# Asking for the first prompt tile's queries and keys during the decoding batch's attention

## The chip, the core and the metric

The kernel runs on one core of one Trainium2 chip. The metric is the device time of one execution in microseconds. The core's engines run side by side and wait for each other through semaphores: TensorE (PE, whose weight loads are listed apart as PEld), VectorE (DVE), ScalarE (ACT), GpSimd (POOL), and SyncE (SP), whose queue issues nearly all DMAs of this kernel in program order.

## The reference

One layer of a streaming encoder is computed for a prompt of 2048 tokens and for a decoding batch of 8 sequences with 16 tokens each. Cut to what matters here:

```python
qm, km, vm, om, ip, fp, qa, ka, va = split_in(x @ w_in)      # one input projection
hm, C1, n1, m1 = mlstm_chunkwise(qm, km, vm, logi, logf, C0, n0, m0, mchunk)
qa = rope(qa.reshape(B, T, A_Q_HEADS, A_HEAD_DIM), pos)      # 8 query heads, 2 key heads of 64
ka = rope(ka.reshape(B, T, A_KV_HEADS, A_HEAD_DIM), pos)
ha = swa_prompt(qa, ka, va, attn_sinks)                      # prompt: window of 128 before the own chunk
ha = swa_step(qa, ka, va, k_cache, v_cache, attn_sinks)      # decoding batch: against its cache
mix = jnp.concatenate([hm, ha], axis=-1) @ w_out
h = layer_norm(DEEPNORM_ALPHA * x + mix, ln1_g, ln1_b)
f, conv_rows = conv_ffn(h, conv_prev, w_up, w_conv, b_conv, w_down)
y = layer_norm(DEEPNORM_ALPHA * h + f, ln2_g, ln2_b)
```

## The kernel before, in words

The 2176 tokens are 17 tiles of 128: prompt tiles 0 to 15, and tile 16, the decoding batch. The program has three large parts: the input projection, the output projection with the first norm, and the feed-forward part. The input projection goes over four blocks of tiles (`IBLOCKS`, the first is tiles 0 to 3 and 16), and over five groups of columns in each. Its results go to DRAM tiles: `zqa` holds a tile's rotated queries of the attention, `zkv` its keys and values, `zqk`, `zv` and `zog` what the mLSTM needs.

Every float32 operand of the large products is split into two parts, a rounded one and the rest (`split`, lines 219 to 221): ScalarE casts the first part, VectorE subtracts it to get the second. The weights come by DMA (`wraw<-wi`, `wraw<-wg`, or already split from DRAM as `w<-zws`), are split a few products ahead, and are consumed from a ring of buffers. `wg` (L469) are the gate and key columns; its four pieces of a block are used by the direct products of line 760. The down-projection's row sums (`txy<-wdn`, lines 874 to 886) are prepared on the side in the same part.

Between the matmuls of the projection TensorE does the work of three chains, written as generators and advanced by `Chains.weave`: `t_sample` for the decoding batch, `m_chain` for the mLSTM of the prompt tiles, `a_chain` for their attention. A chain's `yield cost, delay` says how much TensorE time its step takes and how much later its next step may come, both in the program's own reckoning in nanoseconds. Only the order of TensorE is fixed by this. The order on VectorE, ScalarE, GpSimd and SP is set by a list scheduler, which takes the instructions with their buffers and dependences and orders each engine by its own reckoning of when they can run.

The attention of one prompt tile begins with `swa_dma(t)` (line 1248), which loads the queries into the buffer `qa` (one copy, L1251) and keys and values into `kva` (three copies, L1253). `swa_first` then calls `swa_load`, where TensorE transposes the queries (`pq`, L1261) and keys (`pk`, L1263), and ScalarE and VectorE split them. For later tiles the load of the next tile is issued within the attention of the one before; for tile 0, `a_chain` issues it itself once the decoding batch is done (`chains.done["s"]`) and comes back 4500 later:

```python
if self.a_load is None and self.a_first is None:
    self.a_load = self.swa_dma(t)
    yield 0, 4500
yield from self.swa(t)
```

The attention of the decoding batch, `swa_sample` (line 1493), goes over two halves of four sequences: scores (L1522, L1523), softmax, transposes (L1540, L1541), products with the values (L1549, L1551), copied into `mixa` (L1552). The store of `mixa` (`mix_out`, L1197) is its last step. It has read its own queries from the same buffer `qa` at its start.

Of the kernel before, what the change touches and what calls it, by code (L numbers as in the profile page):

```python
# [204 lines left out]
class Prog:  # L205
# [1060 lines left out]
    def a_chain(self):  # L1266
        self.a_load = self.a_first = None
        while not self.chains.done["s"]:
            yield 0, 500
        for t in range(NPT):  # L1270
            while self.i_done <= self.place(t)[0]:
                yield 0, 500
            if self.a_load is None and self.a_first is None:
                self.a_load = self.swa_dma(t)
                yield 0, 4500
            yield from self.swa(t)
            self.chains.done["a"] = t
# [215 lines left out]
    def swa_sample(self, load, kvc):  # L1493
        nc, a = self.nc, self.a
        V = nc.vector
        t = NPT
        kv, pq, pk = self.swa_load(load)
        nc.sync.dma_start(a["kv_s"], kv)

        qs = self.work("qh", [P, DB, 64], name="qs")  # L1500
        V.tensor_copy(qs.rearrange("p b (j l) -> p j b l", j=4), pq.rearrange("p j (b l) -> p j b l", b=DB))
        ks = self.work("ql", [P, P], name="ks")
        V.tensor_copy(ks, pk)
        yield 550, 3500
        mix = self.work("mixa", [P, 4, P])
        NK = P + DS
        HB = DB // 2
        sk = self.sinkx.to_broadcast([P, HB])
        for half in range(2):
            bs = slice(half * HB, half * HB + HB)  # L1510
            kc, vc = kvc
            vn = self.work("pth", [DS, HB, P], bufs=2, name="vn")
            nc.sync.dma_start(vn, self.zkv[t][half * 64:half * 64 + 64, P:].rearrange("(b l) e -> l b e", b=HB))
            sc = self.work("sc", [P, HB, NK], bufs=2, name="scs")
            mx, es, sm = [self.work(n, [P, HB], bufs=2) for n in ("amx", "aes", "asm")]
            for b0 in (0, 2):
                ps = self.bank([P, 2, NK], "pscs")
                for i in range(2):
                    b = half * HB + b0 + i
                    for kvh in range(2):  # L1520
                        rs = slice(64 * kvh, 64 * kvh + 64)
                        nc.tensor.matmul(ps[rs, i, :P], qs[rs, b], kc[rs, b0 + i], start=True, stop=True)  # L1522
                        nc.tensor.matmul(ps[rs, i, P:], qs[rs, b], ks[rs, b * DS:(b + 1) * DS], start=True, stop=True)  # L1523
                V.tensor_reduce(mx[:, b0:b0 + 2], ps, axis=AX.X, op=ALU.max)
                V.tensor_copy(sc[:, b0:b0 + 2], ps)
            V.scalar_tensor_tensor(mx, mx, 0.125, sk, op0=ALU.mult, op1=ALU.max)
            V.tensor_sub(es, sk, mx)
            nc.scalar.activation(es, es, AF.Exp)
            V.tensor_scalar_mul(mx, mx, -1.0)
            for b in range(HB):  # L1530
                nc.scalar.activation(sc[:, b], sc[:, b], AF.Exp, bias=mx[:, b:b + 1], scale=0.125, accum_out=sm[:, b:b + 1])
            V.tensor_add(sm, sm, es)
            V.reciprocal(sm, sm)
            nc.gpsimd.tensor_mul(sc, sc, sm.rearrange("p (b o) -> p b o", o=1).to_broadcast([P, HB, NK]))
            yield 2700, 6500
            pts = self.work("pth", [P, 2, HB, P], bufs=2, name="pts")
            pp = self.bank([P, HB, P], "ppt")
            pp2 = self.bank([DS, HB, P], "ppt2")
            for i in range(HB):
                nc.tensor.transpose(pp[:, i], sc[:, i, :P], self.ident)  # L1540
                nc.tensor.transpose(pp2[:, i], sc[:, i, P:], self.ident)  # L1541
            nc.scalar.copy(pts[:, 0], pp)
            nc.scalar.copy(pts[:DS, 1], pp2)
            yield 860, 2500
            po = self.bank([P, HB, 64], "ppo")
            halves = [slice(64 * kvh, 64 * kvh + 64) for kvh in range(2)]
            for b in range(HB):
                for cs in halves:
                    nc.tensor.matmul(po[cs, b], vc[:, b, cs], pts[:, 0, b, cs], start=True, stop=False)  # L1549
                for cs in halves:  # L1550
                    nc.tensor.matmul(po[cs, b], vn[:, b, cs], pts[:DS, 1, b, cs], start=False, stop=True)  # L1551
            nc.scalar.copy(mix.rearrange("p j (b l) -> p j b l", b=DB)[:, :, bs], po.rearrange("p b (j l) -> p j b l", j=4))  # L1552
            if half == 0:
                kvc = self.swa_cache(1)
            yield 1900, 500 if half else 7000
        self.mix_out(t, 4, mix)
# [619 lines left out]
```

## Time and profile before

| | |
|---|---|
| time, median of 3 runs | 2326.87 us (2325.21 to 2328.39) |
| time of the profiled execution | 2326.59 us |
| its span | 2324.8 us |
| granted TensorE clock, mean | 0.996 |
| instructions | 39933 |
| busy: PE, DVE, ACT, POOL | 98%, 77%, 56%, 11% |
| chain that ended last: PE, DVE, DMA, ACT | 78%, 7%, 4%, 2% |
| HBM read, written | 451.78 MB, 170.56 MB |

The span runs from the first instruction to the last; the remaining 1.8 us of the profiled execution lie around it. Times of rows are microseconds from the start of the span. In a row of instructions stand start, duration, engine, line, operation, out<-in, size and count; in brackets the engine's idle time before it and what ended it. A row of the list of waits has total time, number, and longest. The granted clock is the share of full speed at which the matmul clock was let run. SPq rows are the queue's issues; a load is there only when it has landed, some us later.

### The profile page before, as it was taken

What the parts mean: (1) busy time and instruction counts of PE and PEld (TensorE: products, weight loads), DVE (VectorE), ACT (ScalarE), POOL (GpSimd) and SP (SyncE); (2) the same over time, 40 slices, a digit from 0 to 9 for tenths busy, and PEclk for the clock granted to TensorE, in tenths of its full rate; (3) what the DMA queues carried; (4) which work ended last, traced back from release to release, by engine and by line L of the source; (5) the groups of instructions that cost most, each with busy time, mean ns of one, the idle gap of its engine ahead of it and who ended that gap; (6) DMA issues with size and microseconds to landing.
All of it is one profiled execution on the core that took longest, in us unless ns stands there. A gap on an engine that the chain in (4) does not pass through costs nothing.

```text
span 2324.8 us, 39933 instructions
## 1 busy us (share of the span) xinstructions
PE 2282.6 (98%) x14425; PEld 2104.6 (91%) x14425; DVE 1801.6 (77%) x3148; ACT 1304.3 (56%) x2465; POOL 244.3 (11%) x298
## 2 busy tenths in 40 slices
PE   9989999999999999999999999999999999999998
PEld 8989988899987777999999999999999988888887
DVE  8677586787678888987888766778766787796897
ACT  5353466676666665655556455556555644554653
POOL 0101101101111221300002000002000000000100
PEclk9999999999999999999999999999999999999999
DMA  7888889889977667787776899887998886756753
GB/s 275 276 309 287 284 294 328 292 279 330 307 254 259 210 212 242 262 321 283 287 272 252 273 319 323 307 309 264 324 298 265 246 284 224 244 197 216 244 189 109
DMA packets 297365, 624.98 MB, mean 269 GB/s; under 512 B 47052, under 2 KB 140240, under 8 KB 297168
## 3 DMA queue, kind: packets, MB, share of 16 engines
q1 hardware_dynamic: 296304, 619.29, 77.8%
q10 hardware_dynamic: 864, 3.15, 0.4%
q8 instruction: 114, 1.87, 0.3%
q14 instruction: 83, 0.68, 0.1%
HBM read 451.78 MB, written 170.56 MB: 268 GB/s over the span
## 4 chain that ended last, share of the span: by engine, by line
PE 78%; DVE 7%; DMA 4%; ACT 2%; issue 2%; SPq 0%; POOL 0%; DVEq 0%; ACTq 0%; POOLq 0%
PE dps L1880 18%; PE fup L1880 18%; PE dps L735 11%; PE dps L2084 6%; PE fht L2084 5%; PE fup L2084 5%; PE dps L225 2%; PE dps L760 2%; PE dps L227 1%; PE dps L226 1%; PE ppo L1371 1%; DVE w L221 1%; PE psc L1322 1%; DMA txy<-wdn 1%; PE ppt L1365 1%
## 5 line engine op out<-in xcount | busy, mean ns | idle before, releaser
L1880 PE MATMUL dps<-hh,uw 128*128 128x384 f32 (+1 forms) x1848 | 477.5, 327 | 5.3 <-DVE u L1913 2.6
L1880 PE MATMUL fup<-hh,uw 128*128 128x384 f32 (+1 forms) x1848 | 476.5, 326 | 0.0
L1928 DVE SCALAR_TENSOR_TENSOR cc<-u,cw,cc 128x768 f32<-128x768 f32 (+1 forms) x264 | 257.8, 978 | 125.1 <-ACT cc L1926 121.7
L1880 PEld LDWEIGHTS dps<-hh,uw 128*128 128x128 f32 x1848 | 329.4, 188 | 7.6 <-DVE u L1913 3.2
L1880 PEld LDWEIGHTS fup<-hh,uw 128*128 128x128 f32 x1848 | 329.4, 188 | 0.0
L1880 PE MATMUL fup<-hl,uw 128*128 128x384 f32 (+1 forms) x924 | 301.3, 326 | 1.1 <-DVE hl L221 1.1
L1880 PE MATMUL dps<-hl,uw 128*128 128x384 f32 (+1 forms) x924 | 301.0, 326 | 0.0
L735 PE MATMUL dps<-w,oh 128*128 128x256 f32 x1344 | 253.4, 284 | 10.1 <-ACT zev L801 5.4
L221 DVE TENSOR_TENSOR w<-wraw,w 128x1024 fp32r<-128x1024 f32 (+2 forms) x163 | 187.9, 1158 | 61.9 <-ACT w L220 59.5
L735 PEld LDWEIGHTS dps<-w,oh 128*128 128x128 f32 x1344 | 211.4, 190 | 23.1 <-issue 9.8
L220 ACT CAST w<-wraw 128x1024 fp32r<-128x1024 f32 (+2 forms) x163 | 161.1, 995 | 124.4 <-PE dps L735 52.2
L220 ACT CAST uw<-wraw 128x1024 fp32r<-128x1024 f32 x126 | 123.3, 982 | 173.7 <-PE dps L2084 104.2
L221 DVE TENSOR_TENSOR uw<-wraw,uw 128x1024 fp32r<-128x1024 f32 x126 | 142.6, 1132 | 63.9 <-ACT uw L220 63.8
L735 PE MATMUL dps<-w,ol 128*128 128x256 f32 x672 | 187.3, 279 | 0.0
L1926 ACT ACTIVATE cc<-u,cw 128x768 f32<-128x768 f32 (+1 forms) x132 | 132.0, 1000 | 96.5 <-DVE u L1922 93.3
L735 PE MATMUL dps<-oh,w 128*128 128x256 f32 x896 | 171.4, 285 | 4.9 <-ACT oh L580 1.7
L1880 PEld LDWEIGHTS fup<-hl,uw 128*128 128x128 f32 x924 | 173.5, 188 | 1.9 <-DVE hl L221 1.9
L1880 PEld LDWEIGHTS dps<-hl,uw 128*128 128x128 f32 x924 | 173.5, 188 | 0.0
L2084 PE MATMUL fup<-uw,fu 128*128 128x512 f32 x726 | 169.0, 389 | 0.0
L2084 PEld LDWEIGHTS fup<-uw,fu 128*128 128x128 f32 x726 | 136.2, 188 | 28.2
L2084 PE MATMUL dps<-uw,fu 128*128 128x512 f32 x660 | 161.0, 389 | 0.1
L735 PEld LDWEIGHTS dps<-oh,w 128*128 128x128 f32 x896 | 141.3, 189 | 11.0 <-issue 4.1
(336 smaller groups left out, 4601.0 us busy)
## 6 DMA issues: line engine op xcount, KB each, us to landing
uw<-zw SPq DMA_DIRECT2D x176, 512.0 KB, 5.1
zw<-uw SPq DMA_DIRECT2D x88, 512.0 KB, 2.9
w<-zws SPq DMA_DIRECT2D x72, 512.0 KB, 6.5
wv<-wup SPq DMA_DIRECT2D x66, 512.0 KB, 6.0
wraw<-wi SPq DMA_DIRECT2D x64, 512.0 KB, 5.0
wraw<-zt SPq DMA_DIRECT2D x60, 512.0 KB, 4.5
wraw<-wdn SPq DMA_DIRECT2D x45, 512.0 KB, 3.8
wraw<-wo SPq DMA_DIRECT2D x40, 512.0 KB, 4.7
```

Of the source, the lines that this page charges most:

```text
L220: nc.scalar.copy(hi, src)
L221: nc.vector.tensor_sub(lo, src, hi.bitcast(F32))
L225: mm(out, ah, bh, start=start, stop=False)
L226: mm(out, ah, bl, start=False, stop=False)
L227: mm(out, al, bh, start=False, stop=stop)
L735: mm(o, l, r, start=s in (1, 7) and c == k == i == 0, stop=k == 3 and i == 2, skip_group_check=True)
L760: mm(o, x, w, start=k == i == 0, stop=k == KD - 1 and i == 2, skip_group_check=True)
L1322: nc.tensor.matmul(ps[kvh][:, j, :nk], q[rs, j0 + j], k[rs, sel], start=i == 0, stop=i == 2)
L1880: mm(ps, l[:, k], r[:, k], start=s in (1, 7) and k == 0 and i == 0, stop=k == 3 and i == 2, skip_group_check=True)
L1926: S.activation(c[:, v], u[:, v, 2:2 + n], AF.Identity, bias=w[3], scale=w[2])
L1928: V.scalar_tensor_tensor(c[:, v], u[:, v, i:i + n], w[i], c[:, v], op0=ALU.mult, op1=ALU.add)
L2084: mm(ps, l[:, k, c], r[:, k], start=s in (1, 4, 7) and u == 0 and k == 0 and i == 0, stop=u == nu - 1 and k == n - 1 and i == 2, skip_grou ...
```

## The change

`swa_sample` issues the load of prompt tile 0 itself, in its second half, after the softmax's last step (a multiplication on GpSimd) is written and before the pause ahead of the transposes. `a_chain` keeps its pause of 4500 for tile 0, but takes the load that is there instead of issuing one.

```diff
@@ a_chain
-            if self.a_load is None and self.a_first is None:
-                self.a_load = self.swa_dma(t)
+            if self.a_first is None and (t == 0 or self.a_load is None):
+                self.a_load = self.a_load or self.swa_dma(t)
                 yield 0, 4500
             yield from self.swa(t)
@@ swa_sample
             V.reciprocal(sm, sm)
             nc.gpsimd.tensor_mul(sc, sc, sm.rearrange("p (b o) -> p b o", o=1).to_broadcast([P, HB, NK]))
+            if half:
+                self.a_load = self.swa_dma(0)
             yield 2700, 6500
```

TensorE's instructions stand in the same order as before. On the other engines the scheduler orders some stretches anew, from the second half of the decoding batch's attention to about the end of the second input block (some 85 rows of SP, 105 of VectorE, 36 of ScalarE and 5 of GpSimd differ); behind that all orders are the same again.

SP's queue, from the load of the second half's new values (`vn`) to the load of tile 0's queries; `wg` are gate weights, `wi` and `zws` projection weights, `zog` and `zv` stores of projection results, `zmix` the store of the batch's attention. Before:

```order
L1513 DMA vn<-zkv_159 16x4x128
L783 DMA zog_113<-zev 128x256
L783 DMA zog_114<-zev 128x256
L494 DMA w<-zws_3_91 128x1024 x2
L906 DMA ropet<-rope 128x192
L469 DMA wraw<-wg 128x528
L1116 DMA qk<-zqk_68 128x8x128
L469 DMA wraw<-wg 128x528
L783 DMA zv_98<-zev 128x256
L783 DMA zv_99<-zev 128x256
L462 DMA wraw<-wi 128x1024
L1197 DMA zmix_160<-mixa 128x4x128
```

Behind these stand `v` (L1118), `og` (L1121) and then `qa<-zqa_126` (L1251). The same stretch now:

```order
L1513 DMA vn<-zkv_159 16x4x128
L1251 DMA qa<-zqa_126 128x512
L783 DMA zog_113<-zev 128x256
L783 DMA zog_114<-zev 128x256
L494 DMA w<-zws_3_91 128x1024 x2
L906 DMA ropet<-rope 128x192
L1116 DMA qk<-zqk_68 128x8x128
L469 DMA wraw<-wg 128x528
L1197 DMA zmix_160<-mixa 128x4x128
L783 DMA zv_98<-zev 128x256
L783 DMA zv_99<-zev 128x256
L469 DMA wraw<-wg 128x528
```

The load of the queries stands right behind `vn`, fourteen issues or more earlier. The store of `mixa` has moved ahead of the two `zv` stores and of the fourth `wg` load, which it stood behind.

VectorE, around the split of tile 0's queries and keys (`ql`, `kringl`), where the last of the gate weights' four splits (`w`, 128x2x264), a projection weight's split (`w`, 128x1024) and two operations on the next block's input (`ol`, `xr`) stand next to it. Before:

```order
L1110 TENSOR_TENSOR mc<-r_b,r_M 4x1
L221 TENSOR_TENSOR w<-wraw,w 128x2x264
L221 TENSOR_TENSOR w<-wraw,w 128x1024
L581 TENSOR_TENSOR ol<-xr,oh 128x1024
L568 TENSOR_TENSOR xr<-xr,wraw 128x1024
L221 TENSOR_TENSOR ql<-pq,qh 128x512
L221 TENSOR_TENSOR kringl<-pk,kringh 128x128
L1133 TENSOR_TENSOR dt<-pm,k_mcau 128x512
L1056 COPY col<-pcol 128x40
L807 TENSOR_TENSOR zev<-dps,zev 128x512
```

Now:

```order
L1110 TENSOR_TENSOR mc<-r_b,r_M 4x1
L221 TENSOR_TENSOR w<-wraw,w 128x2x264 x2
L221 TENSOR_TENSOR ql<-pq,qh 128x512
L221 TENSOR_TENSOR kringl<-pk,kringh 128x128
L581 TENSOR_TENSOR ol<-xr,oh 128x1024
L221 TENSOR_TENSOR w<-wraw,w 128x1024
L568 TENSOR_TENSOR xr<-xr,wraw 128x1024
L1056 COPY col<-pcol 128x40
L1133 TENSOR_TENSOR dt<-pm,k_mcau 128x512
L807 TENSOR_TENSOR zev<-dps,zev 128x512
```

The split of the queries and keys has moved ahead of `ol`, `w` and `xr`, and both last gate splits stand ahead of it.

VectorE some 50 us later, at the third batch of the down-projection's row sums (`txy`), beside the scores of an attention tile (`sc`, `amx`) and the next mLSTM tile (`dt`, `col`). Before:

```order
L805 TENSOR_SCALAR zev<-dps,zev 128x512
L880 TENSOR_TENSOR txy<-txy 128x512
L221 TENSOR_TENSOR w<-wraw,w 128x1024
L1133 TENSOR_TENSOR dt<-pm,k_mcau 128x512
L1056 COPY col<-pcol 128x40
```

Now, from the same row on:

```order
L805 TENSOR_SCALAR zev<-dps,zev 128x512
L221 TENSOR_TENSOR w<-wraw,w 128x1024
L1133 TENSOR_TENSOR dt<-pm,k_mcau 128x512
L1056 COPY col<-pcol 128x40
L1340 TENSOR_TENSOR asm<-asm,aes 128x4
L1341 RECIPROCAL asm<-asm 128x4
```

The first operation on `txy` now comes ten rows later, behind the scores' rows and `amx`.

## Prediction

> **What bounds the kernel now.** I read the page's busy times first, then the list of who waited for whom, then the time-ordered rows around the longest wait, and last the busy time and granted clock in short stretches around it.
>
> ```profile
> PE 2282.6 (98%) x14425; PEld 2104.6 (91%) x14425; DVE 1801.6 (77%) x3148; ACT 1304.3 (56%) x2465; POOL 244.3 (11%) x298
> ```
>
> TensorE (PE) is busy 98% of the span, and no other engine comes near. The change issues no matmul more or fewer, so it can only move what TensorE loses by waiting, or by running at a lower clock. Of TensorE's waits these are the first two:
>
> ```profile
> PE dps L735 <- ACT zev L801: 6.1, 5, 2.3
> PE pq L1261 <- DMA qa<-zqa: 4.1, 1, 4.1
> ```
>
> The first is five waits, the second a single one of 4.1 us, the longest of the kernel, and its releaser is the load that the change moves. Here it is on TensorE and on SP's queue:
>
> ```profile
> 297.31 1.09 PE L1261 MATMUL pq<-ident,qa 128*128 128x128 f32 x4 [4.10 <-DMA qa<-zqa]
> ```
> ```profile
> 274.92 0.49 SPq L1513 DMA_DIRECT2D vn<-zkv  x1
> ...
> 286.76 0.33 SPq L469 DMA_DIRECT2D wraw<-wg  x1
> ...
> 290.40 0.39 SPq L1197 DMA_DIRECT2D zmix<-mixa  x1
> ...
> 292.17 0.48 SPq L1251 DMA_DIRECT2D qa<-zqa  x1
> ```
>
> TensorE had come to the transposes of the first prompt tile at 297.31 - 4.10 = 293.21. Their load was issued at 292.17 and let them go at 297.31, 5.14 us later. So the load is issued about 4 us too late, behind the store zmix<-mixa and two more loads.
>
> ```profile
> 293.20:297.30 4.10, 0.01 (x1) 0.02 (x1) 2.14 (x3) 2.48 (x3) 0.00 (x0) 0.99 1.08 359
> 297.30:300.66 3.36, 3.35 (x16) 3.36 (x17) 2.50 (x4) 0.75 (x2) 0.00 (x0) 0.50 0.97 306
> ```
>
> Columns: the stretch, its length, busy time of PE, PEld, DVE, ACT and POOL, the granted clock, the DMA share, GB/s. The wait has a tail: in the 3.36 us after it the clock is 0.50, so 3.36 x 0.50 = 1.68 us more are lost. The prize is 4.10 + 1.68 = 5.78 us.
>
> **The change part by part.** *The load itself.* It now stands right behind vn<-zkv, so it is issued at 274.92 + 0.49 = 275.4, and with the 5.14 us of before it lands near 280.5, 12.7 us ahead of 293.21. Two things could hold it back on SP's in-order queue: its source has to be stored, and its buffer has to be read by the decoding batch's own transposes.
>
> ```profile
> 242.72 0.44 PE pq L1261 x4
> ```
> ```profile
> 253.94 1.69 SPq L783 DMA_DIRECT2D zqa<-zev  x2
> ```
>
> The first row is from the chain of waits. Both lie 19 us or more ahead, so the queue is not blocked. The issue takes 0.48 us of SP at either place: I cost it at nothing, covered by those 12.7 us; if a load behind it were late, the price would be between 0 and 0.48. The keys' load (L1253) keeps its place. TensorE's order being the same, the transposes now start at 293.21: -4.10, and with no gap ahead of them the half clock goes too: -1.68.
>
> *What else moved: the gate weights.* The scheduler put the store zmix<-mixa ahead of the fourth piece of the gate weights, wraw<-wg. SP takes its work in order, and the store waits for ScalarE (ACT):
>
> ```profile
> 287.34 0.37 ACT L1552 COPY mixa<-ppo 128x256 f32<-128x256 f32 x1 [0.58 <-PE ppo L1551]
> ```
> ```profile
> DMA to landing us min/median/max: 4.9/4.9/4.9
> ```
>
> The second row is that of the line of the wg loads (L469). The store can go at 287.71, and with it and two zv stores in front the piece is issued near 289.2 instead of 286.76; it lands at 289.2 + 4.9 = 294.1. ScalarE casts it, then one zev copy, then qh, in this order in both kernels' queue except for two longer casts that now stand behind:
>
> ```profile
> 291.66 0.64 ACT L220 CAST w<-wraw 128x528 fp32r<-128x528 f32 x1
> ...
> 294.90 0.58 ACT L793 COPY zev<-dps 128x512 f32<-128x512 f32 x1
> ...
> 298.43 0.59 ACT L220 CAST qh<-pq 128x512 fp32r<-128x512 f32 x1 [2.00 <-PE pq L1261]
> ```
>
> So qh is done at 294.1 + 0.64 + 0.58 + 0.59 = 295.9. Behind it stands VectorE (DVE), whose next pieces in the new order are ql, kringl, ol, w, xr, col, dt, zev:
>
> ```profile
> 295.03 1.23 DVE L221 TENSOR_TENSOR w<-wraw,w 128x1024 fp32r<-128x1024 f32 x1 [1.75 <-ACT w L220]
> 296.46 1.23 DVE L581 TENSOR_TENSOR ol<-xr,oh 128x1024 fp32r<-128x1024 f32 x1 [0.20 <-ACT oh L580]
> 297.72 1.22 DVE L568 TENSOR_TENSOR xr<-xr,wraw 128x1024 f32<-128x1024 f32 x1
> 299.05 0.69 DVE L221 TENSOR_TENSOR ql<-pq,qh 128x512 fp32r<-128x512 f32 x1
> 299.66 0.28 DVE L221 TENSOR_TENSOR kringl<-pk,kringh 128x128 fp32r<-128x128 f32 x1
> 302.33 0.69 DVE L1133 TENSOR_TENSOR dt<-pm,k_mcau 128x512 f32<-128x512 f32 x1 [2.39 <-PE pm L1128]
> 302.94 0.19 DVE L1056 COPY col<-pcol 128x40 f32<-128x40 f32 x1
> 303.72 0.69 DVE L807 TENSOR_TENSOR zev<-dps,zev 128x512 f32<-128x512 f32 x1 [0.59 <-PE dps L735]
> ```
>
> These eight take 1.23 + 1.23 + 1.22 + 0.69 + 0.28 + 0.69 + 0.19 + 0.69 = 6.22 us, so zev is done near 302.1, or 301.5 with the overlap of neighbouring starts that the rows show. TensorE needs it: zev is the last reader of the bank into which the second gate product of the next block goes.
>
> ```profile
> 306.42 0.40 PE L760 MATMUL dps<-w,oh 128*128 128x264 f32 x2
> ```
>
> That matmul would come at 306.42 - 5.78 = 300.64. The new wait is 0.9 to 1.5 us, nearest 1.3: +1.3. If the piece lands 1.3 us sooner it is nothing; each us later adds one.
>
> *VectorE lags on.* VectorE is now some 2.5 us earlier than before and TensorE 4.5. The next product of VectorE that TensorE takes with little to spare is sd:
>
> ```profile
> 327.25 0.68 DVE L1156 TENSOR_TENSOR sd<-pscore,dt 128x512 f32<-128x512 f32 x1
> ```
> ```profile
> 328.37 0.38 PE L1233 MATMUL pnum<-v,sd 128*128 128x129 f32 x2
> ```
>
> It is ready at 327.93, 0.44 ahead of its matmul. With a lag of 2.0 us that would be a wait of up to 1.6; what VectorE catches up on the way bounds it below at 0. I take the middle, +0.8.
>
> *Later waits.* Three waits for ScalarE follow in the same input block, and ahead of two of them VectorE stood still for a load of the down-projection's rows:
>
> ```profile
> 337.25 0.39 PE L735 MATMUL dps<-oh,w 128*128 128x256 f32 x1 [1.50 <-ACT zev L793]
> ```
> ```profile
> 355.11 0.69 DVE L880 TENSOR_TENSOR txy<-txy 128x512 f32<-128x512 f32 x1 [3.98 <-DMA txy<-wdn]
> ```
> ```profile
> 366.63 0.39 PE L735 MATMUL dps<-w,oh 128*128 128x256 f32 x1 [1.54 <-ACT zev L793]
> ```
> ```profile
> 392.19 0.69 DVE L881 TENSOR_TENSOR txy<-txy 128x512 f32<-128x512 f32 x1 [4.54 <-DMA txy<-wdn]
> ```
> ```profile
> 402.76 0.38 PE L735 MATMUL dps<-w,oh 128*128 128x256 f32 x1 [1.12 <-ACT zev L801]
> ```
>
> In the new order the txy of 355.11 stands behind dt and col, for which ScalarE's next chain waits, so that chain is freed of most of the 3.98 us, and the wait of 1.54 goes: -1.5. The first and the third are loops between TensorE and ScalarE or keep a txy in front: 0 each, between -1.5 and +1 (a txy load that is issued later).
>
> *Sum.* -4.10 - 1.68 + 1.3 + 0.8 - 1.5 = -5.18 us. The profiled execution took 2326.59 us, 0.28 below the median of 2326.87, so 2326.59 - 5.18 = 2321.4 there and 2321.7 as a median: -0.22%. From about 480 us on the order is the same and TensorE bounds, so what is gained by then stays.
>
> [...] How long may a new wait be before it costs the half clock as well?
>
> ```profile
> 117.15:119.47 2.32, 0.00 (x0) 0.00 (x1) 0.51 (x1) 1.58 (x3) 0.47 (x1) 1.00 0.98 377
> 119.75:123.16 3.41, 3.41 (x18) 3.41 (x18) 3.14 (x4) 2.05 (x3) 0.00 (x0) 0.50 0.91 291
> ...
> 1593.60:1597.00 3.40, 3.40 (x21) 3.40 (x22) 3.40 (x3) 0.66 (x2) 3.33 (x1) 1.00 0.38 136
> ```
> ```profile
> 1593.60 0.44 PE L1880 MATMUL dps<-hh,uw 128*128 128x384 f32 x1 [1.71 <-DVE u L1913]
> ```
>
> After a gap of 2.32 us the clock was 0.50; after one of 1.71 us, that which ends at 1593.60, it was 1.00. So by the rows a new wait of 1.3 us costs itself alone, and one over 2.3 us another 1.68. [...]
>
> **The rivals.** *All of it.* VectorE keeps up and all three later waits go: 5.78 + 1.50 + 1.54 + 1.12 = 9.94, 2316.9 us. For it: VectorE waits 2.39 us for pm now, room to follow. Against: the fourth gate piece is later in the new queue, and two of the three waits have nothing that removes them.
>
> *Eaten up, or not doing what it says.* The gate piece lands 1.5 us later than reckoned: wait 2.8, half clock 1.68, sd 0.8, no later gain: -5.78 + 5.28 = -0.5, 2326.4 us. From a landing at 295.3 on the wait passes 2.3 us and this decides. The same result comes if the transposes find another late partner. For it: the store ahead of the piece; against: it is one load with 4.9 us each time.
>
> *Slower.* The txy loads are issued further back in SP's queue, and VectorE's stalls for them reach TensorE in full. Of 3.98 and 4.54 us only 1.54 and 1.12 did; in full that is 5.86 more, and with gaps over 2.3 us twice 1.68: +9.22. Kept of the gain are 5.78 - 2.1 = 3.68, so +5.5 us, 2332.4. It needs both stalls in front of work that TensorE takes at once; against it speaks that the first now has dt and col ahead of it.
>
> **How the numbers follow.** Two tenths of a per cent, 4.65 us, is about what a measurement of this kernel can tell from no change: 2322.2 and 2331.5 are the bounds. The forecast, between 2319.5 and 2322.2: 0.45. All of it, below 2319.5: 0.13. Eaten up in part or whole, 2322.2 to 2331.5: 0.28. Slower: 0.14. So faster 0.58, same 0.28, slower 0.14. The range 2316.5 to 2328.0 leaves out the slower case and the edges of the next.
>
> **What would show it.** In the changed profile the wait before pq is gone, the half clock after it too, and qa is issued near 275.4. Right on the hand-back: the L760 matmul near 301 waits about 1.3 us for zev (L807), and wg is issued near 289. Right on the later part: one wait of 1.5 us fewer between 330 and 410. Wrong: a gap over 2.3 us with a clock of 0.50 behind it anywhere before 480 us, or TensorE still idle ahead of pq for another cause.

## The result, and the profile after

The changed kernel took 2318.79 us (median of 9 executions, 2315.54 to 2324.8) against 2328.76 us for the kernel before (median of 9, 2325.21 to 2331.78): ratio 0.9958, 95% interval 0.9947 to 0.9969, that is 0.42% less time, 7 to 12 us. A second measurement of the same two, reported below, gave 0.9968 (0.9956 to 0.9980). The forecast was 2321.7 us, 0.22% less.

The profiled execution took 2323.55 us with a span of 2321.3 us, so it is 4.8 us above the median of its kernel, while the one of before, 2326.59 us, is 2.2 us below its own. The two spans differ by 3.5 us only, and the sum cannot be read from them. It has to be read from the stretch that the change touches.

The list of TensorE's waits (engine, line, what it waited for: total us, times, longest) no longer has an entry for `pq`:

```profile
PE dps L735 <- ACT zev L801: 4.7, 4, 1.9
PE dps L760 <- DVE ol L581: 2.7, 1, 2.7
PE dps L1882 <- DVE u L1915: 2.6, 2, 1.7
```

SP's queue in the changed kernel, in order of time, from the new values of the batch to the fourth piece of the gate weights:

```profile
276.10 0.48 SPq L1513 DMA_DIRECT2D vn<-zkv  x1
276.63 0.47 SPq L1251 DMA_DIRECT2D qa<-zqa  x1
...
287.00 0.33 SPq L469 DMA_DIRECT2D wraw<-wg  x1
288.49 0.37 SPq L1197 DMA_DIRECT2D zmix<-mixa  x1
288.95 1.26 SPq L783 DMA_DIRECT2D zv<-zev  x2
290.30 0.40 SPq L469 DMA_DIRECT2D wraw<-wg  x1
```

The load is issued 17.2 us ahead of the transposes, which now follow the matmul ahead of them at once:

```profile
293.68 0.28 PE L735 MATMUL dps<-w,oh 128*128 128x256 f32 x1
293.80 0.60 PE L1261 MATMUL pq<-ident,qa 128*128 128x128 f32 x4
```

and in the two stretches where TensorE stood still and then ran at a clock of 0.50, it is busy throughout at 1.00 (columns as before: stretch, length, busy PE, PEld, DVE, ACT, POOL, clock, DMA share, GB/s):

```profile
293.80:297.20 3.40, 3.40 (x30) 3.20 (x28) 1.95 (x4) 3.10 (x6) 0.00 (x0) 1.00 0.94 295
297.20:300.66 3.46, 3.46 (x29) 3.40 (x29) 3.46 (x5) 1.79 (x3) 0.00 (x0) 1.00 0.78 273
```

**Where the time went.** TensorE's order is the same in both kernels, so the same two matmuls can be timed in each: the one behind the last wait for `w<-zws` near 260 us, and the first product of line 1371 near 775 us, where the orders are one again. Worked out from the traces of two executions of each kernel (idle: gaps of 0.2 us and more between them; half clock: time at 0.50):

| | from | to | time | idle | half clock |
|---|---|---|---|---|---|
| before | 261.12 | 779.34 | 518.22 | 10.87 | 3.41 |
| before, second profile | 260.44 | 778.01 | 517.57 | 9.97 | 3.41 |
| after | 261.85 | 773.58 | 511.73 | 5.59 | 0 |
| after, second profile | 259.67 | 770.42 | 510.75 | 4.52 | 0 |

The means are 517.90 and 511.24: the change takes 6.7 us out of this stretch, 5.4 of idle time and 3.41 x 0.50 = 1.7 of half clock. These make 7.1; some 0.4 is lost again between the starts of matmuls, in delays that show as no gap of 0.2 us. That is the change. What the first profile of the changed kernel loses again lies 800 us later, where the two orders are the same:

```profile
1587.62 0.44 PE L1882 MATMUL dps<-hh,uw 128*128 128x384 f32 x1 [1.75 <-DVE u L1915]
```
```profile
1585.87:1587.62 1.75, 0.00 (x1) 0.00 (x1) 1.75 (x4) 1.75 (x3) 1.42 (x2) 1.00 0.81 297
1588.18:1591.59 3.41, 3.41 (x13) 3.41 (x12) 3.41 (x3) 0.18 (x1) 3.41 (x1) 0.50 0.09 34
```

This wait stands in both kernels (1.71 us before, 1.75 here), but here the clock was 0.50 behind it. In the second profile of the changed kernel, the same wait again, the clock stayed at 1.00:

```profile
1585.35 0.44 PE L1882 MATMUL dps<-hh,uw 128*128 128x384 f32 x1 [1.73 <-DVE u L1915]
```
```profile
1586.55:1589.96 3.41, 3.41 (x24) 3.41 (x23) 3.41 (x4) 1.75 (x3) 3.41 (x1) 1.00 0.37 116
```

So that part is chance, and not the change.

### The profile page after: what moved, and what is told of

Same layout as the page of the kernel before. It is cut to its first block, busy times and chain, and to the rows that moved or that the text cites. A ratio compares the mean times of both kernels' runs of the same rounds, so it can differ in the third digit from the quotient of the medians.

```text
span 2321.3 us, 39923 instructions
## 1 busy us (share of the span) xinstructions
PE 2284.8 (98%) x14425; PEld 2105.7 (91%) x14425; DVE 1802.6 (78%) x3148; ACT 1304.0 (56%) x2465; POOL 245.1 (11%) x298
## 4 chain that ended last, share of the span: by engine, by line
PE 75%; DVE 8%; DMA 6%; issue 3%; ACT 3%; POOL 1%; SPq 0%; DVEq 0%; ACTq 0%; POOLq 0%
PE fup L1882 18%; PE dps L1882 18%; PE dps L735 9%; PE dps L2086 6%; PE fht L2086 5%; PE fup L2086 5%; PE dps L225 1%; PE dps L760 1%; PE dps L227 1%; PE dps L226 1%; PE ppo L1371 1%; DVE w L221 1%; PE psc L1322 1%; PE ppt L1365 1%; DMA w<-zws 1%
```

## The experiments

Each was timed beside the kernel before on the same chip; ratios are against that kernel. One that has another order is judged twice: by its times, and by its time between the two matmuls of the table above (517.9 before, 511.2 after), which leaves out chance elsewhere. A single profile of it carries some 0.5 us either way, as the two pairs show, and more where the half clock falls by chance. The intervals of the ratios are some 0.002 wide or more, so the times tell most of these kernels from the kernel before, but hardly from the changed kernel or from each other.

### Both kernels a second time

No edit.

> The kernel before, a second time, for a second profile and for the clock of each execution. The pair of profiles differs by 3.5 us, the medians by 9.8. Theory: all executions of one kernel have the same waits within 0.5 us, and differ by how many stretches of 3.41 us fall to a clock of 0.50 (1.7 us each); so the wait at pq is 4.1 us again, with a half clock behind it, and over the executions the span falls by about 2.3 us for each 0.001 of mean clock. The profiled execution of before (2326.6) was a lucky one, the median 2328.8 has one stretch more. Rival: executions differ by waits for loads; then spans at the same mean clock differ by 3 us and more.

> The changed kernel, a second time. Median 2317 to 2321 us, ratio 0.995 to 0.997. Theory: up to 780 us the order of events repeats the first profile within 0.5 us: no wait at pq, 1.5 us near 333, 0.3 near 361, none near 396; the half clock at 1588 and the wait of 0.70 at 1685.5, which before did not have, are chance and can be absent, which would make a span near 2317. Rival: they belong to the change and come again.

Measured: the kernel before against itself 1.0002 (0.9989 to 1.0015), 2327.47 and 2327.27 us; the changed kernel 2319.09 us, ratio 0.9968 (0.9956 to 0.9980). The second profile of before has the wait at `pq` (3.35 us) and one half clock behind it; the second of after has neither, and neither the wait of 0.70 at 1685.5 nor the half clock at 1588, so those two belong to the execution, not to the change.

Over all executions of the two (100 of before, from the runs of this study, 19 of after) the span follows the mean clock. For before the spans average 2330.0 us at a mean clock of 0.994 (12 executions), 2325.2 at 0.996 (30) and 2321.7 at 0.998 (3): some 2.2 us for each 0.001. The changed kernel has 2319.0 at 0.996 (5) and 2315.2 at 0.998 (9). At equal clock the kernels differ by about 5.8 us; the mean clock, 0.99568 and 0.99711, makes another 0.00143 x 2.2/0.001 = 3.1 us, which is nearly two stretches of half clock. One is the stretch behind `pq`. The other is not in any of the four profiles; with a scatter of 0.001 from one execution to the next, 19 executions leave the difference uncertain by about 0.0003, or 0.6 us, and whether the rest is chance or a wait that is sometimes longer stays open. The mean clock accounts for somewhat more than half of the variance of the 100 spans of before. At equal clock they still scatter by about 2 us (the 30 at 0.996 lie between 2321.8 and 2328.9), so for that part the rival of the expectation, waits that differ, is not excluded.

### The load in time, with another order behind it

The load stands one line later, after the pause:

```diff
-            if half:
-                self.a_load = self.swa_dma(0)
             yield 2700, 6500
+            if half:
+                self.a_load = self.swa_dma(0)
```

> The load is issued after the pause, ahead of the second half's transposes, not before it. In SP's queue it stands behind two more stores and two more loads (issue near 280, landing near 285, still 8 us ahead of the transposes), the fourth gate piece stands ahead of the store of mixa, and the third batch's first txy operation is ahead of w, dt and col again, as before the change. Theory (the landing in time pays 5.8 us; the order of txy pays the 1.2 to 1.5 us near 361 and the 1.1 near 396): no wait at pq, no half clock behind it, but a wait of about 1.5 us near 361 again; median 1 to 3 us above the changed kernel's. Rival 1 (only the load counts): the same time as the changed kernel's within 1 us. Rival 2 (the new order on the other engines is the gain): within 3 us of before.

Measured: 2323.65 us, ratio 0.9987 (0.9974 to 0.9999), 4.6 us above the changed kernel's second median (the two intervals just touch); between the two matmuls 512.20. In its profile the load is issued at 275.42 and nothing waits at `pq`, and the two later waits are back:

```profile
356.08 0.39 PE L735 MATMUL dps<-w,oh 128*128 128x256 f32 x1 [1.00 <-ACT zev L793]
```
```profile
392.19 0.39 PE L735 MATMUL dps<-w,oh 128*128 128x256 f32 x1 [1.10 <-ACT zev L801]
```

That agrees with the theory: the load's landing pays at `pq`, and the later waits come with the old order of `txy` on VectorE (other rows moved too, so that `txy` is their cause is argued). The time rose more than the 1 to 3 us expected; the trace holds 1.0 of it, and the mean clock of its executions, 0.9959 against 0.9971, stands for another 0.0012 x 2.2/0.001 = 2.6. What lowers that clock is not known: the one profile is of the fastest of its executions, 2316.14 us.

### The load twice, without the landing in time

The load of the change is added to the kernel before, and the old one kept; the transposes wait for the old one:

```diff
+            if half:
+                qx = self.work("qa", [P, 512])
+                nc.sync.dma_start(qx, self.zqa[0])
             yield 2700, 6500
```

> The queries are loaded twice: once where the change loads them, and once more where the kernel before does; the transposes use the second. The queue has the new order around the gate pieces (store of mixa ahead of the fourth), so everything of the change is there but the landing in time. Theory: the wait at pq stays near 4 us and the half clock behind it too; the hand-back stays hidden behind that wait; 2326 to 2330 us, ratio 0.999 to 1.001. Rival (the order of the other engines brings the gain): 2322 to 2324, ratio near 0.998.

Measured: 2326.89 us, ratio 0.9994 (0.9980 to 1.0007). The wait is there, and so is the half clock behind it:

```profile
294.38 0.63 PE L1261 MATMUL pq<-ident,qa 128*128 128x128 f32 x4 [3.31 <-DMA qa<-zqa]
```
```profile
295.62:299.04 3.42, 3.42 (x17) 3.20 (x16) 1.71 (x3) 0.18 (x2) 0.00 (x0) 0.50 0.96 325
```

Without the landing in time there is no measurable gain. But it does not have everything of the change: SP's order around the gate pieces is that of the change, while on VectorE the third batch's first `txy` operation stands ahead of `w`, `dt` and `col`, as before. So it does not test the change's whole order alone. Between the two matmuls it took 515.1, 2.8 us less than before: its redrawn order removed the waits near 402 and 639 and shortened the one near 366. By its trace the rival has a point: an order can be worth 2.8 us by itself. The times do not show it, since its mean clock was lower, 0.9950.

### The wait kept, but filled with work

Sixteen products of the identity with itself are put ahead of tile 0's transposes in the kernel before, so that TensorE works where it waited. They give no part of the result. Cut to the loop (`fill` is a new argument, 16 for tile 0 and 0 for the others):

```diff
+        for j in range(fill):
+            nc.tensor.matmul(pq[:, j % 4], self.ident, self.ident, start=True, stop=True)
         for j in range(4):
             nc.tensor.transpose(pq[:, j], qa[:, j * P:(j + 1) * P], self.ident)
```

> The kernel before, with 16 extra products of the identity with itself (about 3.5 us of TensorE) written ahead of tile 0's transposes, into their own bank, which the transposes then write over; they give no part of the result. TensorE works where it waited for qa. Behind the transposes the scheduler orders some rows anew, up to there nothing moves. Over 45 and 19 executions before and after differ by 8.2 us: 5.5 at equal mean clock, and 0.0014 of mean clock, which is 3.2 us or 1.9 stretches of half clock. Theory 1 (the idle of the one wait pays for one stretch): the transposes end as late as before, but the clock after them is 1.00 and the mean clock rises by 0.0007; about 1.7 us below before. Theory 2 (the one wait pays for nearly two stretches): the mean clock rises by 0.0014, 3.2 us below before. Rival (the half clock there is not due to the idle time): the clock behind the transposes is 0.50 again and the time that of before or more.

Measured: 2326.58 us, ratio 0.9995 (0.9984 to 1.0006). The transposes come as late as before, 3.8 us behind the filling's start, and the clock behind them is 1.00 (the sixteen products are 32 records of the trace):

```profile
293.65 3.73 PE L1261 MATMUL pq<-ident 128*128 128x128 f32 x32
297.44 0.66 PE L1263 MATMUL pq<-ident,qa 128*128 128x128 f32 x4
```
```profile
293.65:297.44 3.79, 3.74 (x35) 3.55 (x33) 1.96 (x3) 2.48 (x3) 0.00 (x0) 1.00 0.87 303
297.44:300.85 3.41, 3.41 (x28) 3.21 (x28) 2.94 (x4) 0.76 (x2) 0.00 (x0) 1.00 0.67 187
```

So the half clock here was the price of the idle time, as the 1.68 of the forecast says. Between the two matmuls it took 516.9, 1.0 us less than before and not 1.7, since behind it the idle gaps make 7.5 us against 6.7: waits of 2.43 us at 337 and 1.05 at 356 are longer or new there. The times cannot tell one stretch from two, and the mean clock, 0.9968, lies between the two theories.

### The load much earlier

```diff
-            if half:
+            if not half:
                 self.a_load = self.swa_dma(0)
```

> The load is issued in the first half of the batch's attention, some 24 us earlier than in the changed kernel (issue near 252). SP's order around the gate pieces is that of before (the fourth piece ahead of the store of mixa), the third batch's first txy operation stands behind dt and col as in the changed kernel. Theory: no wait at pq, no half clock behind it; the small hand-backs of the changed kernel (0.2 for zev near 301, 0.4 for sd near 324) are gone and the wait near 361 stays short: 0 to 1.5 us below the changed kernel, 2317 to 2319.5. Rival (earliness itself costs: the load collides with others near 252): a new wait between 250 and 262, at or above the changed kernel's time.

Measured: 2321.41 us, ratio 0.9979 (0.9966 to 0.9992); between the two matmuls 513.4. The load costs nothing where it is issued (248.46), and nothing waits at `pq`. The loss is elsewhere: at the matmul where I had forecast a wait of 1.3 us for the changed kernel there is one of that size here, by another cause. The chain of waits of this kernel from ScalarE's cast to TensorE (start, us, what):

```profile
291.65 1.05 ACT w L220
292.69 0.49 ACT qh L220
293.18 0.17 ACT kringh L220
293.35 0.49 ACT zev L793
293.84 0.96 ACT oh L580
...
297.82 0.69 DVE zev L807
298.51 0.04 issue
298.56 0.51 PE dps L760 x2
```

ScalarE takes `w` ahead of `qh` here, `ql`, `ol` and `xr` of VectorE follow, `zev` is done at 298.51, and the product of line 760 waits 1.49 us for it. The gate piece is not late here, since its store order is that of before. In the changed kernel `qh` goes ahead of that `w`, and 0.21 us remain. The third batch's `txy` stood behind `dt` and `col`, as expected, and the wait near 361 was gone; that near 402 was back (1.12 us at 393.9), and another of 1.03 us at 407.8.

### The load at its old place, in another queue

One word for tile 0, in the kernel before:

```diff
-        nc.sync.dma_start(qa, self.zqa[t])
+        (nc.scalar if t == 0 else nc.sync).dma_start(qa, self.zqa[t])
```

> The kernel before with one word changed: tile 0's queries are loaded at their old place in the program, but by ScalarE's queue instead of SP's. Theory (the load was late because it stood behind the stores and loads of SP's in-order queue): ScalarE issues it after the copies of mixa near 288 or earlier, it lands by 293, and the wait at pq falls under 1 us or away; with the txy order of the changed kernel 2318 to 2322. Rival (it was late because of its place in the program): it is issued near 292 again and the wait is 4 us as before, 2326 to 2329.

Measured: 2320.89 us, ratio 0.9981 (0.9971 to 0.9991). The program's place is unchanged, and the load is issued at 241.5, 50 us earlier than before. The scheduler put it in ScalarE's queue right behind the decoding batch's own transposes (240.85, 0.60 us), which read the same buffer:

```profile
L1251 ACTq DMA_DIRECT2D qa<-zqa x1: 338/338/338, 241.5 to 241.5; - x1
```

The wait at `pq` is gone. So the place in SP's in-order queue made the load late, and not the place in the program alone; I had expected 288, and missed how free ScalarE's queue is. Between the matmuls it took 514.1: a wait of 2.48 us at 331.7 (1.50 before), with a half clock behind it, took back part of the gain.

### Without the pause

The changed kernel, which for tile 0 no longer pauses by 4500 if the load is there. This moves some rows of TensorE too.

```diff
+                new = self.a_load is None
                 self.a_load = self.a_load or self.swa_dma(t)
-                yield 0, 4500
+                if new:
+                    yield 0, 4500
```

> The changed kernel, without the pause of 4500 that a_chain still makes for tile 0 although the load is there: tile 0's transposes and all of its attention come earlier in TensorE's order. Theory: nothing waits for the load in the changed kernel any more (13 us of reserve), so the pause buys nothing, and TensorE bounds: the same time as the changed kernel's within 1.5 us. Rival (the moved rows meet ScalarE and VectorE at the gate pieces): waits of 1 to 3 us between 288 and 310, 2321 to 2324.

Measured: 2324.17 us, ratio 0.9984 (0.9975 to 0.9994). No wait between 288 and 310, so the rival has it wrong; the theory misses too, since the time is 5 us above the changed kernel's medians. TensorE is idle for only 3.5 us between the two matmuls, the least of all, yet it took 515.3, since 13.65 us of it ran at half clock. The first of it lies where TensorE's order is that of all the kernels:

```profile
256.24:259.65 3.41, 1.49 (x11) 1.11 (x10) 1.56 (x2) 1.70 (x3) 0.00 (x0) 1.00 1.02 357
259.65:263.06 3.41, 3.41 (x28) 2.72 (x27) 0.00 (x0) 0.00 (x0) 0.00 (x0) 0.50 0.97 357
263.06:266.48 3.42, 3.42 (x25) 2.95 (x26) 0.00 (x0) 0.37 (x1) 0.00 (x0) 0.50 0.62 231
266.48:269.89 3.41, 3.41 (x18) 3.41 (x18) 1.08 (x2) 1.22 (x2) 0.00 (x0) 0.50 0.43 138
```

The half clock follows two waits for weights of 1.24 and 0.68 us (1.03 and 0.65 at the same matmuls before), and the clock stays low for three stretches, for which I have no reason. What the pause itself is worth is therefore not settled; dropping it brought no gain.

### Own buffers for the row sums

`txy` shares its buffers with the input tiles (`xr1`, `xr3`). Here it gets two of its own, in the kernel before and in the changed one:

```diff
-... name="txy", tag=f"xr{q}", bufs=1) for q in (1, 3)]
+... name="txy", tag=f"txy{q}", bufs=1) for q in (1, 3)]
```

> The kernel before, but the down-projection rows (txy) get two buffers of their own instead of two of the input's, so that their loads need not wait for those to be read and are issued earlier. Theory (VectorE's stalls for txy cause the waits of 1.5 us near 366 and 1.1 us near 402): the two stalls of 4.0 and 4.5 us of VectorE are gone, the two waits with them, the wait at pq of 3.3 to 4.1 us stays with its half clock: 2.7 us less, 2324.5. Rival (those waits are loops of TensorE and ScalarE that do not hang on txy): the stalls go and waits of 1 us or more remain near 366 and 402, same time as before. Either way the order on the other engines changes elsewhere too, which can add a wait of 1 to 2 us.

> The same buffers in the changed kernel. Theory: its third and fourth batch no longer reach TensorE there, so the buffers bring nothing more: 2317 to 2321, and the two kernels with own buffers differ by the load alone, 5.8 us in the traces (4.1 of wait, 1.7 of half clock). Rival (the order that came with the change is what counts): the two kernels with own buffers differ by less than 3 us.

Measured: 2332.16 us, ratio 1.0016 (1.0002 to 1.0029), in the kernel before; 2331.32 us, 1.0014 (0.9999 to 1.0029), in the changed one. Both theories fall here, and of the second expectation the rival holds: the medians of the two kernels differ by 0.8 us. With the buffers free earlier the scheduler redraws the whole first part. In the kernel before, the two waits went as expected, and others came, the longest of 3.05 us at 450. In the changed kernel the wait at `pq` is gone as everywhere, and waits of 2.43, 1.28, 3.45 and 3.11 us stand at 335, 366, 404 and 458. That at 404 comes by the mechanism of the slower rival of the forecast, a stall of VectorE for `txy`. SP's queue, then rows of the chain of waits of this kernel:

```profile
389.92 0.41 SPq L1197 DMA_DIRECT2D zmix<-mixa  x1
390.37 0.50 SPq L875 DMA_DIRECT2D txy<-wdn  x1
```
```profile
390.37 5.68 DMA txy<-wdn
396.06 0.02 issue
396.08 0.70 DVE txy L881
...
401.42 1.23 ACT sc L1337 x5
...
403.59 0.48 ACT zev L801
404.07 0.04 issue
404.11 1.01 PE dps L735 x3
```

The load of `txy` stands behind the store of the attention's result, VectorE waits 5.04 us for it, the scores behind it come late, so ScalarE's exponentials and then `zev`, and TensorE waits 3.45 us and runs 6.8 us at half clock. So the load in time was there, its prize too, and an order drawn worse elsewhere took all of it. (This profile, 2337.15 us, lies 5.8 us above its kernel's median.)

## Why the prediction was right, and where its terms were off

The direction, the place and the prize were right: the wait at `pq` and the half clock behind it are gone, in both profiles after and in each kernel with the load in time. The time lies in the range, 3 us below the forecast. It is also below 2319.5, in the part that the forecast gave to "all of it" with a chance of 0.13. The trace accounts for 6.7 us of the difference, so two errors of size, hand-backs that did not come and later waits that fell by more, went the same way; the 1 to 3 us beyond were forecast by no term, and that they bring the time close to that rival's is luck. Point by point:

- **The load.** Issue at 276.63, forecast 275.4; the program runs 0.7 us later there (261.85 against 261.12 at the first matmul of the table). Nothing holds it up, and up to 775 us no matmul behind it waits for a load in either profile of after. The row at 253.94 that I named as the store of its source is not that one: the kernels with the earlier load and the other queue issue it at 248.5 and 241.5, ahead of that row's place. The queue was free all the more. The -4.10 was 4.10 in one profile of before and 3.35 in the other, the -1.68 was 1.7 in both.
- **The gate weights, +1.3: mis-sized.** The order of events was as forecast, store ahead of the piece, piece issued at 290.30, then `qh`, `ql`, `zev`. The wait was 0.21 us in one profile and under 0.2 in the other:

```profile
294.10 0.63 ACT L220 CAST w<-wraw 128x528 fp32r<-128x528 f32 x1 [1.66 <-DMA wraw<-wg]
...
295.12 0.59 ACT L220 CAST qh<-pq 128x512 fp32r<-128x512 f32 x1
```
```profile
295.74 0.69 DVE L221 TENSOR_TENSOR ql<-pq,qh 128x512 fp32r<-128x512 f32 x1 [0.26 <-ACT qh L220]
...
300.97 0.68 DVE L807 TENSOR_TENSOR zev<-dps,zev 128x512 f32<-128x512 f32 x1
```
```profile
301.71 0.51 PE L760 MATMUL dps<-w,oh 128*128 128x264 f32 x2 [0.21 <-DVE zev L807]
```

  The piece landed 3.8 us after its issue and not 4.9, `qh` ended at 295.71, 0.9 us sooner than reckoned when the 0.7 us of offset are taken off, and neighbouring operations of VectorE overlap, so that `zev` ended at 301.65 where 5.91 us, not 6.22, had passed since `ql`. TensorE came at 301.50. That this chain can hold up this matmul is shown by the kernel with the earlier load, 1.49 us there, though by a longer cast ahead of `qh` and not by a late piece.
- **VectorE's lag, +0.8: mis-sized.** `sd` ended 0.06 us ahead of its matmul in one profile, and in the other the matmul waited 0.38 us for it.

```profile
323.09 0.68 DVE L1156 TENSOR_TENSOR sd<-pscore,dt 128x512 f32<-128x512 f32 x1
```
```profile
323.83 0.49 PE L1233 MATMUL pnum<-v,sd 128*128 128x129 f32 x2
```

- **The later waits, -1.5: right for the one, too small by the other.** The wait of 1.54 fell to 0.32, that of 1.50 stayed, both as forecast:

```profile
332.95 0.39 PE L735 MATMUL dps<-oh,w 128*128 128x256 f32 x1 [1.51 <-ACT zev L793]
```
```profile
361.37 0.39 PE L735 MATMUL dps<-w,oh 128*128 128x256 f32 x1 [0.32 <-ACT zev L793]
```
```profile
388.78 0.69 DVE L880 TENSOR_TENSOR txy<-txy 128x512 f32<-128x512 f32 x1 [2.02 <-DMA txy<-wdn]
```

  The wait of 1.12 near 402, which I had left at 0, went as well: VectorE's stall ahead of it fell from 4.54 to 2.02 us. Across the kernels this stall and that wait go together: 4.5 and 4.7 us of stall with 1.12 and 1.26 us of wait (before), 3.8 + 1.4 with 1.12 and 1.15 (the load much earlier, the other queue), 2.6 with 1.10 (the load one line later), 5.0 with 3.45 (own buffers), 2.0 with none (after, twice), 1.6 and 2.5 with none (the load twice, the filled wait), 2.0 with 0.47 (without the pause). That the stall is the cause is argued from this and not shown by a run that moves it alone. Some of it came back as 0.47 us near 409 and as other waits under 0.75. Of the idle time behind 302 us, 5.4 us before and 3.5 after, 1.9 are gone; the two terms together had said 0.7.
- **The sum.** -3.7 at `pq`, -1.7 of clock, 0.1 at the gate weights, -1.9 later and 0.4 of small delays make -6.8; the table says -6.7, the forecast said -5.2. The rest of the measured difference, 1 to 3 us, is the mean clock of the executions, not a wait of the two pairs of profiles.
- **The rivals.** "All of it" was nearest in time, but not by its mechanism: one of its three waits stayed. "Eaten up" needed the gate piece to land 1.5 us later than reckoned; it landed at 294.10, as reckoned, and 0.7 us sooner by the program's own time. "Slower" needed the loads of `txy` further back, and was met not by this change but by the same change with own buffers, which between the two matmuls took 524.5 us against 520.8 for the kernel before with own buffers, though its prize at `pq` is in it (6.8 us of half clock stand in the one, 1.7 in the other).
- **The rule on the clock was too simple.** I took from two rows that a gap of 1.71 us costs no clock and one of 2.32 does. The same gap did and did not, as shown above: behind 1.75 us in the first profile of after the clock was 0.50, behind 1.73 us in the second 1.00. Read to the letter, its sign of being wrong is met as well: a gap of 2.68 us ends at 163.32 in the changed kernel, and the clock behind it is 0.50 (164.83 to 168.24). The same gap stands in the kernel before (162.64), with 0.50 behind it too (164.13 to 167.53); the sign could only mean gaps that are new.

## What to carry to other kernels

The load that SP's queue held up here cost its wait, 4.10 and 3.35 us in the two profiles of before, and 1.7 us of half clock behind the wait. Both were gone in each kernel that issued it ahead of the store of `mixa`, which it had stood behind, by its place (276.63 instead of 292.17) or by another queue (241.5). Where a scheduler redraws the other engines, that prize is only one term: six kernels with the load in time took 511.2, 512.2, 513.4, 514.1, 515.3 and 524.5 us for the same work (6.8 us of each of the last two are half clock), and 517.9 without, so a neighbouring place for the same load is worth a trial, and each must be judged on its own trace. With a scatter from one execution to the next as here (2315.54 to 2324.8 us in nine of the changed kernel), a change of this size is read between two fixed matmuls of an unchanged order, not from two spans.

## What the runs showed of the hardware

In these profiles the granted clock was 0.50 behind some waits of TensorE and 1.00 behind others. These are waits that the argument used (a single stretch at 0.50 is 3.41 us long):

| profile | TensorE's wait, us | ended at | clock behind it |
|---|---|---|---|
| before | 2.32, for `zev` (L801) | 119.47 | 0.50, 119.75 to 123.16 |
| before | 2.68, for `ol` (L581) | 162.64 | 0.50, 164.13 to 167.53 |
| before | 4.10, for `qa` at `pq` | 297.31 | 0.50, 297.30 to 300.66 |
| before | 1.71, for `u` | 1593.60 | 1.00, 1593.60 to 1597.00 |
| after | 2.68, for `ol` (L581) | 163.32 | 0.50, 164.83 to 168.24 |
| after | 1.75, for `u` | 1587.62 | 0.50, 1588.18 to 1591.59 |
| after, second profile | 1.73, for `u` | 1585.35 | 1.00, 1586.55 to 1589.96 |
| the load twice | 3.31, for `qa` at `pq` | 294.38 | 0.50, 295.62 to 299.04 |
| the wait filled with work | none at `pq` | | 1.00, 297.44 to 300.85 |
| without the pause | 1.24 and 0.68, for `w` | 258.03 and 259.18 | 0.50, 259.65 to 269.89 |

The length of a wait alone does not tell its price here: the three of 1.71 to 1.75 us stand at the same matmul, and one of them had 0.50 behind it. Nor is the price always one stretch: behind the wait at `pq` there was one in both profiles of before, behind the two waits of the kernel without the pause there were three. What decides in either case is left open here.
